# Changing where halves of weights are made and dealt in a gMLP, attention and PEER block on one core

## The chip, the cores and the metric

The kernel runs on one core of a Trainium2 chip. The metric is the device time of one execution in microseconds (us). Names used below: PE is TensorE (matmuls), DVE is VectorE, ACT is ScalarE, POOL is GpSimd, SP is the engine that issues most loads. Each engine works through a queue of its own in order, and engines wait for one another by semaphores. SBUF is the memory on the chip, PSUM the banks that PE writes its products into.

## What is computed

For 512 tokens of width 1024 in float32:

```python
xn = rms_norm(x, ln_mix_g);  proj = xn @ w_in
a_out = gmlp_spatial_gating(proj[..., :512], proj[..., 512:1024], ...)
b_out = banded_chunk_attention(q, k, v, ...)          # 8 heads, chunks of 64
x = x + concatenate([a_out, b_out]) @ w_out
# PEER: 8 heads, 16 of 128 x 128 experts each
q = rms_norm(x) @ w_query;  sc = q . sub_keys         # two halves of the key
best, eidx = top 16 of the sums of the two top 16
g = softmax(best);  u = expert_u[eidx];  vv = expert_v[eidx]
x = x + sum(g * gelu(u . xn) * vv)
```

There are 16384 experts, and each token uses 8 x 16 of them.

## The kernel before

**Halves.** A float32 product is made of three matmuls of a shorter format. A weight tile of 128 x 1024 is loaded into `raw` (512 KB, SP's queue, three buffers), ACT copies it to `hi` (L157, five buffers), and DVE or POOL subtracts to get `lo` (L158, five buffers). `mm3` (L196 to L198) then multiplies hi by hi, hi by lo and lo by hi. `load_split` (L149) does load, copy and subtraction in one go; `Pieces` (L181) does the same for the first chunks of `w_in`, piece by piece (L140, L145, L146).

**Head.** The first chunk of `w_in` comes in four pieces. Three are loaded at the start (the `raw` buffers), the fourth after the second piece has been used. The product of token tile 0 goes over the pieces as they come (`product`, L339), while PE transposes token tile 1 (L292), DVE multiplies it with the gain (`xg`, L298) and ACT and DVE halve it (`xh` L303, `xl` L304). The first k-steps of tile 1 follow.

**PEER.** 384 of the 512 tokens don't gather their experts: for them the hidden product is made with all 16384 experts, and gates that are zero for all but the chosen ones are multiplied in. (64 of these tokens are handled by gathers all the same, early, in the gate stage; the remaining 128 tokens gather in the loop, spread over DVE and POOL.) The experts come in 128 tiles of 128.

- A *first product* is one tile of experts by 320 tokens: 8 k-steps of 3 matmuls into a PSUM bank (`pu`, two banks). ACT's gelu (L724) moves the bank to `act`. `multiply_some(n)` (L698) issues n k-steps, from a tile left open or from the list `ready`, which holds tiles whose halves have been issued; `HELD` is 2.
- A *second product* (L1171) takes two tiles of `vd` rows (64 chunks, c = 0 to 63) and the gated activations `wh`, `wl` into 6 PSUM banks (L1215). Ahead of it DVE multiplies the gates `gc` in (L1181), ACT and DVE halve the outcome (L1182, L1183).

**Gate stage** (L1029 to L1090, 438.6 to 584.2 us in the trace). The order of PE, DVE, ACT and POOL is written out by hand there. 48 steps of 8 tokens, with a lead of 2: in each step POOL makes `bm` (L981) from two digits `hb` and `lb` of the expert number, DVE makes `am` (L989), PE multiplies them for each token (L998: eight matmuls in the program, 16 records in the trace), ACT copies the four-token results out of two PSUM banks (`gst`, L1001) and, each second step, stores them (`gd`, L1005, 1024 KB). `digits` (L963) makes `hb` (a one-hot, L970, times the gate, L973) and `lb` (L970) for 16 tokens at a time. From step 6 to step 32, in seven steps of eight, POOL also gathers rows for the 64 tokens (`rowe`, L660) and DVE multiplies and sums them (L670). Behind the gate matmuls of a step, `some` k-steps of first products are issued: what is left by then, divided by the steps that are left. At the end of a step the halves of the next tile are issued in one go (load, copy, subtraction; every fourth subtraction on POOL), while `ready` holds fewer than two.

**Loop** (L1225 on). For each c the second product of c and the two first products of c + 25 are issued, and every third c the routing of the gathered tokens on DVE. PE's order is by hand; the other engines' order is set by a scheduler by priority. Only `queued_behind` and `issue_after` tie an instruction to another one's place.

## Time and profile before

| what | value |
|---|---|
| median of three runs | 1411.17 us (1410.4 to 1411.97) |
| the profiled execution | 1410.74 us |
| its span on the core | 1409.0 us |
| granted TensorE clock | 0.999 |
| PE busy | 1386.7 us (98%) |
| DVE busy | 1154.3 us (82%) |
| POOL busy | 673.0 us (48%) |
| ACT busy | 612.0 us (43%) |
| DMA | 396.24 MB, mean 281 GB/s |

The span runs from the first to the last instruction, and all times of rows count from its start. In a timeline a row has the start, the duration, engine, line of the kernel before, operation, what it writes and reads, and in brackets the idle time of the engine ahead of it with what ended that. An x behind a row counts equal instructions in a run. Matmuls overlap, so the pitch between their starts is their price, not the duration.

### The profile page before, as it was taken

Reading aid. Unit: us, or ns where it says so; the run is one execution under the profiler, and the core shown is the slowest. Engines: PE = TensorE matmul, PEld = TensorE weight load, DVE = VectorE, ACT = ScalarE, POOL = GpSimd, SP = SyncE. Lnnn points to the kernel's source line nnn. Section 1 sums busy time; section 2 is a strip of 40 time slices with the busy share of each in tenths; the row PEclk is TensorE's granted clock in tenths of the full one; section 3 lists DMA queues with packets and bytes.
Section 4 is the critical chain, followed back from the end, with each engine's and each line's share of the span. In section 5 each row is a group of like instructions: output and inputs, shape, how many; then the busy total and the mean of one; then the engine's idle time right before and its main releaser. Section 6 shows DMA issues by size and latency. Waiting matters only on the chain.

```text
span 1409.0 us, 21692 instructions
## 1 busy us (share of the span) xinstructions
PE 1386.7 (98%) x7838; PEld 1224.6 (87%) x7838; DVE 1154.3 (82%) x2508; ACT 612.0 (43%) x960; POOL 673.0 (48%) x486
## 2 busy tenths in 40 slices
PE   9999999999999989999999999999999999999998
PEld 7887688899899989988898899899889989888887
DVE  5437845898998998678999999898898887889983
ACT  5447635443434445534344444444443333333331
POOL 0002103777778998424555456454464543344520
PEclk9999999999999999999999999999999999999999
DMA  4452316567666999979999999999999998799981
GB/s 165 135 194 76 104 72 199 193 220 271 240 225 222 348 354 281 289 254 355 330 342 348 362 360 342 369 372 359 375 348 383 352 359 337 272 353 363 357 311 60
DMA packets 164330, 396.24 MB, mean 281 GB/s; under 512 B 12880, under 2 KB 75232, under 8 KB 162176
## 3 DMA queue, kind: packets, MB, share of 16 engines
q1 hardware_dynamic: 64640, 194.14, 37.6%
q0 software_dynamic: 48176, 173.46, 33.9%
q10 hardware_dynamic: 51408, 27.27, 6.6%
q8 instruction: 61, 1.00, 0.3%
q14 instruction: 45, 0.37, 0.1%
HBM read 363.34 MB, written 31.46 MB: 280 GB/s over the span
## 4 chain that ended last, share of the span: by engine, by line
PE 78%; DVE 13%; DMA 2%; POOL 2%; issue 2%; ACT 2%; ACTq 0%; DVEq 0%; POOLq 0%
PE pa L1215 23%; PE px L1215 12%; PE pu L196 9%; PE pu L198 9%; PE pu L197 9%; PE pa L998 3%; PE pa L196 3%; PE pa L197 3%; PE pa L198 3%; DVE rowe L670 2%; DVE lo L158 2%; DVE tree L800 1%; DVE am L989 1%; DMA raw<-in_vd 1%; POOL rowe L660 1%
## 5 line engine op out<-in xcount | busy, mean ns | idle before, releaser
L157 ACT ACTIVATE hi<-raw 128x1024 fp32r<-128x1024 f32 x296 | 313.0, 1058 | 448.2 <-DMA raw<-in_uT 120.8
L158 DVE TENSOR_TENSOR lo<-raw,hi 128x1024 fp32r<-128x1024 f32 x244 | 305.7, 1254 | 99.9 <-ACT hi L157 99.1
L1139 POOL DMA_INDIRECT row<-in_ud,eint x128 | 193.0, 1508 | 180.8 <-DVE acc L1152 129.4
L196 PE MATMUL pu<-xch,hi 128*128 128x320 f32 x784 | 247.5, 316 | 3.0 <-ACT act L724 2.8
L1150 POOL DMA_INDIRECT row<-in_vd,eint x128 | 159.7, 1247 | 178.0 <-DVE row L1141 118.6
L198 PE MATMUL pu<-xch,lo 128*128 128x320 f32 x784 | 242.8, 310 | 0.8 <-DVE lo L158 0.8
L197 PE MATMUL pu<-xcl,hi 128*128 128x320 f32 x784 | 242.8, 310 | 0.0
L1215 PE MATMUL pa<-lo,wh 128*128 128x512 f32 x512 | 199.7, 390 | 0.0
L1215 PE MATMUL pa<-hi,wh 128*128 128x512 f32 x512 | 199.4, 389 | 0.0
L158 POOL TENSOR_TENSOR lo<-raw,hi 128x1024 fp32r<-128x1024 f32 x52 | 124.0, 2398 | 119.0 <-ACT hi L157 116.1
L1152 DVE SCALAR_TENSOR_TENSOR acc<-row,hw,acc 128x1024 f32<-128x1024 f32 x128 | 165.2, 1290 | 2.8 <-DMA row<-in_vd,eint 2.5
L1141 DVE SCALAR_TENSOR_TENSOR row<-row,xb 128x1024 f32<-128x1024 f32 x128 | 155.7, 1220 | 10.3 <-DMA row<-in_ud,eint 10.3
L1215 PE MATMUL pa<-hi,wl 128*128 128x512 f32 x512 | 158.5, 389 | 0.0
L196 PEld LDWEIGHTS pu<-xch,hi 128*128 128x128 f32 x784 | 148.0, 189 | 6.1 <-ACT act L724 4.4
L197 PEld LDWEIGHTS pu<-xcl,hi 128*128 128x128 f32 x784 | 148.1, 189 | 1.4
L198 PEld LDWEIGHTS pu<-xch,lo 128*128 128x128 f32 x784 | 147.8, 189 | 1.1 <-DVE lo L158 1.0
L1215 PEld LDWEIGHTS pa<-hi,wh 128*128 128x128 f32 x512 | 96.1, 188 | 20.5
L1215 PEld LDWEIGHTS pa<-hi,wl 128*128 128x128 f32 x512 | 96.1, 188 | 20.3
L1215 PEld LDWEIGHTS pa<-lo,wh 128*128 128x128 f32 x512 | 96.1, 188 | 20.2
L998 PE MATMUL pa<-bm,am 128*128 128x128 f32 x768 | 95.1, 277 | 8.0 <-POOL bm L981 4.2
L998 PEld LDWEIGHTS pa<-bm,am 128*128 128x128 f32 x768 | 90.7, 191 | 11.7 <-POOL bm L981 6.5
L1215 PE MATMUL px<-hi,wh 128*128 128x512 f32 x256 | 100.1, 391 | 0.4 <-ACT hi L157 0.4
(236 smaller groups left out, 2641.6 us busy)
## 6 DMA issues: line engine op xcount, KB each, us to landing
raw<-in_uT SPq DMA_DIRECT2D x128, 512.0 KB
raw<-in_vd SPq DMA_DIRECT2D x128, 512.0 KB
gd<-gst ACTq DMA_DIRECT2D x24, 1024.0 KB
gc<-gd SPq DMA_DIRECT2D x15, 1280.0 KB
raw<-in_w_in SPq DMA_DIRECT2D x19, 512.0 KB
raw<-in_wq SPq DMA_DIRECT2D x16, 512.0 KB
raw<-in_w_out SPq DMA_DIRECT2D x8, 512.0 KB
gc<-gd SPq DMA_DIRECT2D x15, 256.0 KB
```

Of the source, the lines that this page charges most:

```text
L157: top = nc.scalar.activation(hi, raw, AF.Copy)
L158: ins = eng.tensor_tensor(lo, raw, hi.bitcast(F32), op=ALU.subtract)
L196: nc.tensor.matmul(ps, lh[0], rh[0], start=first, stop=False)
L197: nc.tensor.matmul(ps, lh[0], rh[1], start=False, stop=False)
L198: nc.tensor.matmul(ps, lh[1], rh[0], start=False, stop=last)
L670: nc.vector.scalar_tensor_tensor(row, row, 1.0, xbu, op0=ALU.mult, op1=ALU.mult, accum_out=du[:, j:j + 1])
L998: nc.tensor.matmul(ps[:, i * P:(i + 1) * P], am[:, 4 * q + i, :], bm[:, 4 * q + i, :], start=True, stop=True)
L1139: nc.gpsimd.indirect_dma_start(out=row, out_offset=None, in_=ud, in_offset=bass.IndirectOffsetOnAxis(ap=eint[:, j:j + 1], axis=0))
L1141: nc.vector.scalar_tensor_tensor(row, row, 1.0, xb0, op0=ALU.mult, op1=ALU.mult, accum_out=hw[:, j:j + 1])
L1150: nc.gpsimd.indirect_dma_start(out=row, out_offset=None, in_=vd, in_offset=bass.IndirectOffsetOnAxis(ap=eint[:, j:j + 1], axis=0))
L1152: nc.vector.scalar_tensor_tensor(acc0, row, hw[:, j:j + 1], acc0, op0=ALU.mult, op1=ALU.add)
L1215: nc.tensor.matmul(accs[t][half], (wh, wh, wl)[k][:, b, tok], w[b][k % 2][:, ds_], start=first and k == 0, stop=last and k == 2)
```

## The change

Four edits in one:

1. The fourth piece of the first `w_in` chunk goes into a raw buffer of its own (`raw3`), and its load is issued right behind that of token tile 1. The load of `qkgt` now comes later on SP's queue.
2. `digits` makes `hb` for 32 tokens in one pair of operations every second time; `lb` stays at 16.
3. In the gate stage a tile's load and copy are issued at the start of a step (`split_begun`), ahead of the gst copies on ACT, and its subtraction at the step's end. It is begun while `ready` holds at most two. The k-steps are dealt out by another formula: steps up to own - 5 (own is 40) count three times as much as those behind. Per step PE's first-product matmuls were 6 once, 9 ten times and 6 for 36 steps; they are now 6 once, 9 for 30 steps, 6 for five, 3 for four and none for the last seven.
4. In the loop each copy `hi` of a half is queued behind the gelu of the half five earlier, where that half was a first product's and its gelu was issued in the loop.

The diff, without the changes that only carry the new entry of a tuple along:

```diff
...
 AHEAD = 25
 LAST = 2
 HELD = 2
+LATE = 3
 EASY = 8
 SOME = 15
 FILL = (0, 1, 2, 3, 4, 4, 3, 3)
...
                        allow_small_or_imprecise_dtypes=True)
 
         loads, splits, ready = [], [], []
+        halves_of, gelus, looping = [0], {}, []
         roots, behind_scale, behind_norm, halved = [], [], [], []
 
         def queued_behind(marks):
...
                 ctx.enter_context(tc.issue_after(i))
             return ctx
 
-        def load_pieces(src, n, b):
-
-            raw, hi, lo = big("raw", F32, RAW), big("hi", F32R, HI), big("lo", F32R, LO)
+        def load_pieces(src, n, b, raw=None):
+
+            raw, hi, lo = raw or big("raw", F32, RAW), big("hi", F32R, HI), big("lo", F32R, LO)
             m = 1024 // n
             cs = [slice(i * m, (i + 1) * m) for i in range(n)]
             for i in range(n):
...
             fold = (lambda v: v.rearrange("p (a b) -> p a b", **dims)) if dims else (lambda v: v)
             load = nc.sync.dma_start(fold(raw), src)
             loads[:] = [getattr(load, "ins", load)]
-            top = nc.scalar.activation(hi, raw, AF.Copy)
+            halves_of[0] += 1
+            with queued_behind(gelus.get(halves_of[0] - HI, [])):
+                top = nc.scalar.activation(hi, raw, AF.Copy)
             ins = eng.tensor_tensor(lo, raw, hi.bitcast(F32), op=ALU.subtract)
             halved[:] = [getattr(i, "ins", i) for i in (top, ins)]
             if eng is nc.gpsimd:
                 splits[:] = [getattr(ins, "ins", ins)]
             return fold(hi), fold(lo)
 
+        def split_begun(i):
+
+            raw, hi, lo = big("raw", F32, RAW), big("hi", F32R, HI), big("lo", F32R, LO)
+            load = nc.sync.dma_start(raw.rearrange("p (a b) -> p a b", b=P), uT[i].rearrange("p (a b) -> p a b", b=P))
+            loads[:] = [getattr(load, "ins", load)]
+            halves_of[0] += 1
+            n_ = halves_of[0]
+            nc.scalar.activation(hi, raw, AF.Copy)
+
+            def finish(eng):
+                eng.tensor_tensor(lo, raw, hi.bitcast(F32), op=ALU.subtract)
+                ready.append((*divmod(i, BC), [v.rearrange("p (a b) -> p a b", b=P) for v in (hi, lo)], n_))
+            return finish
+
         def split_tile(i, eng):
 
-            ready.append((*divmod(i, BC), load_split(uT[i], eng, b=P)))
+            ready.append((*divmod(i, BC), load_split(uT[i], eng, b=P), halves_of[0]))
 
         def chunk_of(w, c, ch=CH, eng=nc.vector, ks=range(KT)):
 
...
             def __init__(self, w, c, first):
                 self.w, self.c, self.first, self.parts = w, c, first, {}
 
-            def load(self, j):
+            def load(self, j, raw=None):
                 self.parts[j] = load_pieces(self.w[2 * j * P:2 * (j + 1) * P, self.c * CW:(self.c + 1) * CW]
-                                            .rearrange("(k p) n -> p k n", p=P), 1 if j else self.first, CW)
+                                            .rearrange("(k p) n -> p k n", p=P), 1 if j else self.first, CW, raw)
 
             def split(self, j, i=0, n=2):
                 self.parts[j][1](i, n)
...
                 for j in range(3):
                     w_at.load(j)
                 nc.sync.dma_start(x_t[1], x_r[1])
+                w_at.load(3, prea.tile([P, D], F32, name="raw3", tag="xs", bufs=4))
                 ps0 = pu()
 
                 def product(t, ps, ks):
...
                 w_at.split(1, 0)
                 w_at.split(1, 1)
                 product(0, ps0, range(2, 4))
-                w_at.load(3)
                 w_at.split(2, 0)
                 w_at.split(2, 1)
                 scale_of(0)
...
         def activate_tile():
-            c, b, ps = begun.pop(0)
+            c, b, n_, ps = begun.pop(0)
             ins = nc.scalar.activation(acts[c][:, b, :], ps[:, :NDU], AF.Gelu_apprx_tanh)
             done[:] = [getattr(ins, "ins", ins)]
+            if looping:
+                gelus[n_] = list(done)
...
             nc.tensor.transpose(ps[:, 3 * P:4 * P], gate[:, t, :], ident)
             return ps.rearrange("p (a t) -> p a t", a=4)
 
+        high = []
+
         def digits(g, q):
 
-            ts_ = slice(q * QT, (q + 1) * QT)
-            hb = gp.tile([P, QT, BH], F32, name="hb", tag="hb", bufs=2)
-            lb = gp.tile([P, QT, BL], F32, name="lb", tag="lb", bufs=2)
-            for i, (d, n) in enumerate(((hb, BH), (lb, BL))):
-                full = [P, QT, n]
+            w = 2 * QT
+
+            def one_hot(name, i, n, ts_):
+                full = [P, ts_.stop - ts_.start, n]
+                d = gp.tile(full, F32, name=name, tag=name, bufs=2)
                 nc.vector.tensor_tensor(d, iota_k[:, None, 0:n].to_broadcast(full),
                                         g[:, 1 + i, ts_, None].to_broadcast(full), op=ALU.is_equal)
-                if i == 0:
-                    nc.vector.tensor_tensor(d, d, g[:, 3, ts_, None].to_broadcast(full), op=ALU.mult)
-            return hb, lb
+                return d
+
+            if q % 2 == 0:
+                ts_ = slice(q * QT, q * QT + w)
+                hb = one_hot("hb", 0, BH, ts_)
+                nc.vector.tensor_tensor(hb, hb, g[:, 3, ts_, None].to_broadcast([P, w, BH]), op=ALU.mult)
+                high[:] = [hb]
+            return high[0][:, q % 2 * QT:(q % 2 + 1) * QT], one_hot("lb", 1, BL, slice(q * QT, (q + 1) * QT))
 
         def second_one_hot(d, c):
 
...
             multiply_tile()
             for n in range(steps + LEAD):
                 t, c = divmod(n, per)
+                halved_now = []
+                if n > 1 and split < (AHEAD - LAST) * BC + HELD and len(ready) <= HELD and (n > EASY or n % 2 == 0):
+                    halved_now = [(split_begun(split), nc.vector if split % 4 else nc.gpsimd)]
+                    split += 1
                 if n < steps:
                     bms[n] = second_one_hot(dgs[n * TC // QT], c)
                 if n >= LEAD:
...
                     t1, c1 = divmod(n + 2, per)
                     dgs[(n + 2) * TC // QT] = digits(late if n + 2 >= own else gs[t1], c1 * TC // QT)
 
-                made = len(ready) * KT + (KT - open_tile[4] if open_tile else 0)
-                left = (AHEAD - LAST) * BC * KT - split * KT + made
-                some = -(-left // (steps + LEAD - n))
+                made = len(ready) * KT + (KT - open_tile[5] if open_tile else 0)
+                left = (AHEAD - LAST) * BC * KT - split * KT + made + len(halved_now) * KT
+                some = -(-left * LATE // (LATE * max(0, own - 5 - n) + min(steps + LEAD - n, steps + LEAD - own + 5)))
                 multiply_some(some)
-                if n > 1 and split < (AHEAD - LAST) * BC + HELD and len(ready) < HELD and (n > EASY or n % 2 == 0):
-                    split_next(nc.vector if split % 4 else nc.gpsimd)
+                for finish, eng in halved_now:
+                    finish(eng)
             while ready or open_tile:
                 if split == AHEAD * BC and not weights:
                     weights[0] = rows_of_v(0)
...
         acx = px()
         accs = [[acx[:, 0:512], acx[:, 512:]]] + [[pa() for _ in range(2)] for _ in range(ND - 1)]
         own_last = []
+
+        looping.append(True)
 
         def second_product(c, between):
             w = weights.pop(c) if c in weights else rows_of_v(c)
```

SP at the head of the program. raw tiles are pieces of `w_in`, x_t token tiles of x, qkgt two small gains. Before:

```order
L140 DMA raw_166<-in_w_in 128x2x512
L140 DMA raw_170<-in_w_in 128x2x512
L336 DMA x_t_114<-in_x 128x1024
L386 DMA qkgt_376<-in_qkg 128x2
L140 DMA raw_198<-in_w_in 128x2x512
L369 DMA x_t_115<-in_x 128x1024
```

After:

```order
L142 DMA raw_166<-in_w_in 128x2x512
L142 DMA raw_170<-in_w_in 128x2x512
L354 DMA x_t_114<-in_x 128x1024
L142 DMA raw3_175<-in_w_in 128x2x512
L387 DMA x_t_115<-in_x 128x1024
L387 DMA x_t_116<-in_x 128x1024
```

The fourth piece (raw_198, now raw3_175) stands right behind x_t_114, token tile 1; qkgt has gone behind the token tiles.

DVE in the middle of the gate stage, two steps. am and the digits hb, lb belong to the gates, rowe to the early gathers, lo to the next first products. Before:

```order
L970 TENSOR_TENSOR hb_5293<-iota_k_74,pa_5077 128x128
L973 TENSOR_TENSOR hb_5293<-hb_5293,pa_5077 128x128
L970 TENSOR_TENSOR lb_5294<-iota_k_74,pa_5077 128x256
L989 TENSOR_TENSOR am_5319<-iota_k_74,pa_5077 128x1024
L670 SCALAR_TENSOR_TENSOR rowe_5171,du_2091<-rowe_5171,px_2074 128x1024
L989 TENSOR_TENSOR am_5346<-iota_k_74,pa_5077 128x1024
L670 SCALAR_TENSOR_TENSOR rowe_5226,du_2091<-rowe_5226,px_2074 128x1024
L970 TENSOR_TENSOR hb_5351<-iota_k_74,pa_5077 128x128
L973 TENSOR_TENSOR hb_5351<-hb_5351,pa_5077 128x128
L970 TENSOR_TENSOR lb_5352<-iota_k_74,pa_5077 128x256
L158 TENSOR_TENSOR lo_5365<-raw_5363,hi_5364 128x1024
```

After:

```order
L992 TENSOR_TENSOR lb_5312<-iota_k_74,pa_5071 128x256
L178 TENSOR_TENSOR lo_5289<-raw_5287,hi_5288 128x1024
L1016 TENSOR_TENSOR am_5339<-iota_k_74,pa_5071 128x1024
L688 SCALAR_TENSOR_TENSOR rowe_5174,du_2091<-rowe_5174,px_2074 128x1024
L1016 TENSOR_TENSOR am_5376<-iota_k_74,pa_5071 128x1024
L688 SCALAR_TENSOR_TENSOR rowe_5240,du_2091<-rowe_5240,px_2074 128x1024
L992 TENSOR_TENSOR hb_5381<-iota_k_74,pa_5071 128x256
L999 TENSOR_TENSOR hb_5381<-hb_5381,pa_5071 128x256
L992 TENSOR_TENSOR lb_5384<-iota_k_74,pa_5071 128x256
L178 TENSOR_TENSOR lo_5357<-raw_5355,hi_5356 128x1024
```

The pair for hb stands in every second group, at twice the size, and in two steps there are two subtractions lo where there was one.

ACT in the loop, around the second product of c = 1 and the first products behind it. hi are copies of halves, act the gelus (pu is the PSUM bank that one frees), wh the halves of gated activations, top a step of the routing. Before:

```order
L1182 ACTIVATE wh_6707<-act_2859 128x2x320
L157 ACTIVATE hi_6576<-raw_6575 128x1024
L1195 ACTIVATE wh_6707<-gc_6065 128x4x2x16
L157 ACTIVATE hi_6626<-raw_6625 128x1024
L157 ACTIVATE hi_6659<-raw_6658 128x1024
L724 ACTIVATE act_6511<-pu_6510 128x320
L724 ACTIVATE act_6219<-pu_6245 128x320
L767 ACTIVATE top_7286<-pos_7287 128x16
L157 ACTIVATE hi_6696<-raw_6695 128x1024
```

After:

```order
L1215 ACTIVATE wh_6671<-act_2859 128x2x320
L161 ACTIVATE hi_6540<-raw_6539 128x1024
L1228 ACTIVATE wh_6671<-gc_6061 128x4x2x16
L161 ACTIVATE hi_6590<-raw_6589 128x1024
L742 ACTIVATE act_6475<-pu_6474 128x320
L161 ACTIVATE hi_6623<-raw_6622 128x1024
L742 ACTIVATE act_6183<-pu_6209 128x320
L742 ACTIVATE act_6475<-pu_6507 128x320
L161 ACTIVATE hi_6660<-raw_6659 128x1024
```

Of the two copies that stood together ahead of two gelus, the second (hi_6659, now hi_6623) stands behind the first gelu.

More of the change, by code (lines that the diff above doesn't have):

```diff
@@ L708, in multiply_some @@
                                                                           tag=f"act{slot}")
-                c, b, (hi, lo), ps, k0 = open_tile
+                c, b, (hi, lo), n_, ps, k0 = open_tile
                 k1 = min(KT, k0 + n)
@@ L713, in multiply_some @@
                 n -= k1 - k0
-                open_tile[4] = k1
+                open_tile[5] = k1
                 if k1 == KT:
-                    begun.append((c, b, ps))
+                    begun.append((c, b, n_, ps))
                     open_tile.clear()
```

## The prediction

> **What bounds the kernel now.** I read the page first, then the waits of TensorE, a table of windows over the stages, and last the timelines around the longest waits and around every place that the change touches.
>
> From the page, the busy time of each engine (PE is TensorE, PEld its weight loads, DVE VectorE, ACT ScalarE, POOL GpSimd; us, share, instructions) and the rate of the DMA by slice:
> ```profile
> PE 1386.7 (98%) x7838; PEld 1224.6 (87%) x7838; DVE 1154.3 (82%) x2508; ACT 612.0 (43%) x960; POOL 673.0 (48%) x486
> GB/s 165 135 194 76 104 72 199 193 220 271 240 225 222 348 354 281 289 254 355 330 342 348 362 360 342 369 372 359 375 348 383 352 359 337 272 353 363 357 311 60
> ```
> PE is busy for 98%, and the change leaves the number of matmuls alone. So it can only win idle time of PE, time at a low clock, or work that hides elsewhere. The longest wait of PE, from the view of its waits (us in total, times, longest):
> ```profile
> PE pu L196 <- ACT act L724: 3.0, 3, 2.0
> ```
> L196 is a first product, which waits until ScalarE's gelu has emptied a PSUM bank. Now the windows: the gate stage from the step where the new dealing of first products begins to differ (473.41) in two parts, the start of the loop over c, and the loop up to 765 us:
> ```profile
> 473.41:537.38 63.97, 57.41 (x451) 54.24 (x449) 63.09 (x99) 29.28 (x50) 60.81 (x39) 1.00 1.06 352
> 537.38:584.24 46.86, 45.42 (x373) 44.92 (x373) 32.47 (x50) 24.48 (x42) 34.90 (x19) 1.00 0.90 264
> 612.60:634.70 22.10, 20.08 (x100) 17.89 (x99) 18.57 (x65) 10.23 (x18) 10.24 (x5) 0.92 0.58 196
> 634.70:765.00 130.30, 130.30 (x710) 117.02 (x708) 126.10 (x325) 54.69 (x85) 67.75 (x48) 1.00 0.93 339
> ```
> Columns: length, then busy time of PE, PE's weight loads, DVE, ACT, POOL, then granted clock, DMA share, GB/s. Each stage has its own limit. In the first row, where the early gathers run, DVE is full (63.09 of 63.97), POOL nearly so (60.81), the DMA at a share of 1.06, and PE idles 6.6 us. In the second PE is the bound (45.42 of 46.86) and DVE and POOL have room. In the third PE idles 2 us and its clock falls to 0.92. In the fourth PE is full, but DVE has only 4.2 us to spare. The dealing moves PE work from the second row into the first: that is the core of the forecast.
>
> **The head: the fourth piece in a buffer of its own.** ScalarE, then VectorE, then PE:
> ```profile
> 13.93 1.15 ACT L145 ACTIVATE hi<-raw 128x512 fp32r<-128x512 f32 x2 [1.53 <-DMA raw<-in_w_in]
> ```
> ```profile
> 14.59 1.29 DVE L146 TENSOR_TENSOR lo<-raw,hi 128x512 fp32r<-128x512 f32 x2 [1.74 <-ACT hi L145]
> 15.80 1.28 DVE L298 TENSOR_TENSOR xg<-pa,g 128x512 f32<-128x512 f32 x2
> ```
> ```profile
> 13.11 1.04 PE L292 MATMUL pa<-ident,x_t 128*128 128x128 f32 x8
> 14.61 0.50 PE L196 MATMUL pu<-hi,xh 128*128 128x512 f32 x1 [0.46 <-ACT hi L145]
> ...
> 17.19 0.50 PE L196 MATMUL pu<-hi,xh 128*128 128x512 f32 x1 [0.44 <-ACT xh L303]
> ```
> The piece lands late, so its hi starts at 13.93 after 1.53 us of waiting, DVE makes lo at 14.59, and only behind that comes xg (15.80), then ScalarE's xh, for which the next product waits until 17.19. With its load issued ahead of the wait for a raw buffer, hi and lo fall before the transposes of 13.11 end (14.15). Then xg starts at about 14.15, and the product 1.39 behind it, as now, at 15.5: 17.19 less 15.5 is **-1.7 us**. It can't gain more than the waits of the chain, 1.53 + 0.46 or 2.0; it gains nothing if x_t[2] and x_t[3], now behind one more load on SP's queue, become what is late. I take 1.7, since those two are used a product later. qkgt, moved behind them too, is read after this product only.
>
> **The gate stage.** A step is 16 gate records and some first-product matmuls. Their prices, on PE:
> ```profile
> 443.22 0.31 PE L197 MATMUL pu<-xcl,hi 128*128 128x320 f32 x1
> 444.31 0.42 PE L198 MATMUL pu<-xch,lo 128*128 128x320 f32 x1 [0.78 <-DVE lo L158]
> 444.57 0.31 PE L196 MATMUL pu<-xch,hi 128*128 128x320 f32 x1
> ...
> 445.45 1.95 PE L998 MATMUL pa<-bm,am 128*128 128x128 f32 x16
> 447.15 0.40 PE L196 MATMUL pu<-xch,hi 128*128 128x320 f32 x1
> ```
> From 444.57 to 445.45 there are six first-product matmuls: 0.147 each. The gate records take 447.15 - 445.45 = 1.70. The code now deals 9 matmuls to each of 30 steps, 6 to five, 3 to four and none to seven; before it was 9 to ten and 6 to 36.
>
> *Begun halves.* hi ahead of the gst copies takes away the wait at 444.31: from 443.22 to 444.31 went 1.09 where 0.15 is the pitch. -0.9; it may gain nothing if lo, now at the end of a step, stays late. Behind the copy on ACT's queue now stand the gst copies, for which PE's gate matmuls wait; the copy is about 1.15 us long (the two halves of 13.93), PE has PSUM banks for two steps, and its raw tile is asked for as soon as a buffer comes free, tiles ahead. So I take nothing for it, up to 1 us a tile if that cover is gone.
>
> *Gather phase (473.41 to 537.38, 20 steps).* Three more matmuls a step are 60, or 8.8 us of PE work, where PE idles 6.6: by PE alone +2.2. But DVE is the fuller engine here. Its rows for this window, then POOL's around 507 and DVE's subtraction beside them:
> ```profile
> L158 DVE TENSOR_TENSOR lo<-raw,hi 128x1024 fp32r<-128x1024 f32 x5 | 9.4, 1877 | 0.0
> L970 DVE TENSOR_TENSOR lb<-iota_k,pa 128x256 f32<-128x256 f32 x10 | 4.1, 413 | 0.0
> L973 DVE TENSOR_TENSOR hb<-hb,pa 128x128 f32<-128x128 f32 x10 | 2.9, 287 | 0.3
> L970 DVE TENSOR_TENSOR hb<-iota_k,pa 128x128 f32<-128x128 f32 x10 | 2.8, 281 | 0.3 <-POOL bm L981 0.3
> ```
> ```profile
> 506.77 1.94 POOL L981 TENSOR_TENSOR bm<-hb,lb 128x1024 f32<-128x1024 f32 x1
> 508.87 1.80 POOL L660 DMA_INDIRECT rowe<-in_ud,eui  x1 [0.16 <-issue]
> ```
> ```profile
> 506.55 3.25 DVE L158 TENSOR_TENSOR lo<-raw,hi 128x1024 fp32r<-128x1024 f32 x1
> ```
> Sixty matmuls are 2.5 tiles more, so 2.5 more halves; three in four fall to DVE: 1.9 x 1.88 = 3.6 us. The digits give back: ten pairs cost 2.9 + 2.8 = 5.7, five pairs of double size at 0.413 each cost 4.1, so -1.6. DVE: +2.0. The DMA: 2.5 x 512 KB = 1.3 MB more at 352 GB/s is +3.7 if it is the limit, and nothing if it can go at the 383 that a later slice shows. Between +2.0 and +3.7 nothing tells them apart; I take **+2.8**.
>
> A half on DVE and a bm on POOL hold each other up: the lo of 506.55 took 3.25 beside the bm of 506.77, where two of half the size took 1.29 at 14.59, and the gather behind it, 508.87, took 1.80. The Trainium skill ("SBUF — State Buffer", "Who interferes with whom") says that a DVE operation with two SBUF inputs and a GpSimd operation take an exclusive lock on a shared port pair, and the loser is blocked to the end of the other; the trace agrees, 1.94 + 1.29 is 3.23. That speaks against three more matmuls a step here, and is a case of its own below.
>
> *Late steps (537.38 to 584.24, 16 steps).* 96 matmuls become 30 + 12 = 42: 54 x 0.147 = -7.9. Seven steps then have 1.70 of PE work, and POOL needs 1.94 for a bm (506.77), so +0.24 each, +1.7. Net -6.2. The 1.4 us of idle left there may go or stay.
>
> *Afterwards.* The gate steps hold 6 + 270 + 30 + 12 = 318 first-product matmuls instead of 312, so six fewer are left for later: -0.9.
>
> Gate stage: -0.9 + 2.8 - 6.2 - 0.9 = **-5.2 us**, from -8.9 (2.2 for the gather phase, and the 1.4 us gone as well) to about 0 (below).
>
> **The loop: halves behind gelus.** ScalarE and PE around the longest wait:
> ```profile
> 627.18 2.00 ACT L157 ACTIVATE hi<-raw 128x1024 fp32r<-128x1024 f32 x2 [1.83 <-issue]
> 629.09 0.74 ACT L724 ACTIVATE act<-pu 128x320 f32<-128x320 f32 x2
> ```
> ```profile
> 629.56 0.41 PE L196 MATMUL pu<-xch,hi 128*128 128x320 f32 x1 [2.02 <-ACT act L724]
> ...
> 631.46 0.47 PE L198 MATMUL pu<-xch,lo 128*128 128x320 f32 x1
> 631.72 0.47 PE L196 MATMUL pu<-xch,hi 128*128 128x320 f32 x1
> ```
> Two copies stand ahead of a gelu that PE waits for. With the gelu first, or between them, the 2.0 us go, and with them what follows: at 631.46 a matmul has a pitch of 0.26 instead of 0.147, for some 13 matmuls: 1.6 us more. Together -3.6.
>
> The page "TensorE: Matmul & The Clock Gate" of the Trainium skill (Part 1) puts the cold clock behind an idle window of about 3.4 us; here 2.0 us of idle went ahead of it. By that page the 1.6 would not hang on this wait and would stay; the forecast's sum would be the same, for the cap below is under 2.0, and the case without a cap 1401.6.
>
> The same place comes once more, with a table load:
> ```profile
> 763.07 1.06 ACT L157 ACTIVATE hi<-raw 128x1024 fp32r<-128x1024 f32 x1 [0.60 <-DMA raw<-in_uT]
> 764.15 1.28 ACT L724 ACT_TABLE_LOAD   x1
> ```
> ```profile
> 765.93 0.42 PE L196 MATMUL pu<-xch,hi 128*128 128x320 f32 x1 [0.73 <-ACT act L724]
> ```
> One copy leaves the place ahead of the load, 1.06 us, more than the 0.73. So -4.3 in sum. But this gain is PE's alone: DVE has 4.2 us to spare up to 765, and further on its subtraction reaches PE just in time:
> ```profile
> 782.97 1.22 DVE L158 TENSOR_TENSOR lo<-raw,hi 128x1024 fp32r<-128x1024 f32 x1
> ```
> ```profile
> 785.41 0.31 PE L198 MATMUL pu<-xch,lo 128*128 128x320 f32 x1
> ```
> lo ends at 784.19 and is read at 785.41: 1.2 us. What PE gains before 612 us moves DVE too, for there DVE follows PE; what it gains behind that can only use up this 1.2, plus a little that DVE's idle 3.5 us in 612.60 to 634.70 may give. I take **-1.5**, between 0 and -4.3. Put behind gelus, the copies come later by at most 0.74, the time of the two gelus of 629.09. Behind a copy stand on ACT the wh copies of the second product, for which DVE and PE wait; a gelu starts when its matmuls end, so they wait no longer than that either, and DVE's full queue covers it.
>
> **Sum:** -1.7 - 5.2 - 1.5 = -8.4. The profiled execution took 1410.74, its span and 1.7 us around it; it is 0.43 under the median of 1411.17. So 1402.3 against it, and **1402.8** as a median. About 0.2%, 2.8 us, is what a measurement can tell from no change.
>
> **The rivals.**
> - *No cap by DVE.* The loop gives all of -4.3: 1400.0. For: DVE's chain up to 634 waits for PE in places, and it may start earlier. Against: 126.10 of 130.30.
> - *The port holds the gather phase.* All subtractions that DVE then does there, three in four of 7.5 or 5.6, take 3.25: 18.2 instead of 9.4 us, less 1.6 of digits and 0.9 of DVE's idle time, +6.3 instead of +2.8: 1406.3. For: 506.55. Against: the mean of 1.88 says that about one in three meets a whole bm.
> - *The copies do nothing in the loop*: the waits move to the next gelu and stay. 1404.3.
> - *The gate stage gains nothing*: both limits add up, the port's 6.3 and the DMA's 3.7 less the 2.0 of DVE that is in both: +8.0 instead of +2.8, -3.2 in sum, 1408.0, or no change where the loop gains nothing either.
> - *Slower: the stores hold the gate results.* ScalarE's waits in the gather phase:
> ```profile
> ACT gst L1001 <- DMA gd<-gst: 4.2, 2, 3.0
> ```
> A copy out of PSUM waits for the store that has its buffer, twice, 2.1 each. With 1.3 MB more on a full DMA all ten stores of the phase could: 8 x 2.1 = +17, in place of +2.8: 1417. It decides against the kernel from 1.4 us a store on ((8.4 + 2.8) / 8). Against it: the loads asked for are 6% more bytes, and the DMA reached 383 GB/s.
>
> **How the numbers follow.** Chances: forecast 0.45, no cap 0.17, port 0.18, nothing in the loop 0.06, gate gains nothing 0.08, stores 0.06. The first four are faster by over 0.2%: 0.86. The fifth lies at the bound: 0.08 the same. The last is 0.06 slower. The range leaves out the stores and half of the fifth above, and below only the corner where every bound comes out good (-1.7 - 8.9 - 4.3 is 1396.3): 1397.0 to 1408.3.
>
> **What would show it.** Right: the product of 17.19 near 15.5; the part that was 473 to 537 some 3 us longer and the part behind it 6 to 7 shorter, first second-product matmul 6 to 8 us earlier; no wait of 2 us and clock 1.00 around 630; instead waits for lo L158 near 750 to 790. Wrong: gate steps over 3.4 us in the gather phase, waits of gst for gd in more than two places, or an idle stretch of PE ahead of the first second product, while gates are loaded.

## The result, and the profile after

The changed kernel took 1399.76 us (median of 4, 1397.34 to 1401.7) against 1411.57 us; the ratio is 0.991 (95% interval 0.9897 to 0.9923), 10.9 to 14.5 us less. In another group of runs it took 1400.74 against 1411.99, 0.9916 (0.99 to 0.9931). The forecast was 1402.8, from 1397.0 to 1408.3: the direction and the range hold, and the change is 3 us larger than the likeliest value. The profiled execution, at 1397.34, is the fastest of its four; where it matters, a second profile of the same kernel, of an execution of 1401.05, stands beside it.

The busy times and the longest waits of PE after:

```profile
PE 1381.2 (99%) x7838; PEld 1222.8 (88%) x7838; DVE 1154.7 (83%) x2484; ACT 615.5 (44%) x960; POOL 672.1 (48%) x486
```

```profile
PE pa L1025 <- DVE ff L909: 1.9, 1, 1.9
PE px L1248 <- ACT hi L161: 1.5, 1, 1.5
PE pu L214 <- ACT act L742: 1.2, 2, 0.8
```

Before, the longest in sum was the one for bm (us in total, times, longest):

```profile
PE pa L998 <- POOL bm L981: 4.2, 8, 1.2
```

The wait of 2.0 us for a gelu is gone, and 0.5 us is left of the 4.2 us for bm. Two waits have grown at their places: PE now waits 1.9 us for the indices ff ahead of the twelfth gate step, where it waited 0.4 (over the stage it is 1.9 in both, in two places before), and 1.5 us instead of 0.4 for a copy hi in the first second product. The gate stage after, cut at the same steps as before, and the place where PE waited at 630 us:

```profile
435.80:471.61 35.81, 33.89 (x275) 33.66 (x273) 33.57 (x44) 20.15 (x32) 33.73 (x22) 1.00 0.89 277
471.61:536.05 64.44, 63.59 (x508) 63.09 (x508) 64.13 (x88) 33.76 (x55) 61.59 (x38) 1.00 1.07 361
536.05:574.49 38.44, 37.78 (x319) 37.19 (x319) 28.08 (x38) 20.70 (x37) 31.83 (x18) 1.00 0.90 261
600.00:621.00 21.00, 20.94 (x117) 18.77 (x116) 18.03 (x65) 10.12 (x18) 7.92 (x4) 1.00 0.63 212
```

In the gather phase (second row) PE was busy for 57.41 of 63.97 us and is now for 63.59 of 64.44: 60 more matmuls were taken up for half a microsecond. Where the 13.7 us between the two spans come from, by the starts of the same instruction in both traces:

| stretch | before | after | difference | second profile | forecast |
|---|---|---|---|---|---|
| up to the first gate matmul | 438.62 | 435.80 | -2.8 | -1.7 | -1.7 |
| first 11 gate steps | 34.79 | 35.81 | +1.0 | +1.0 | -0.9 |
| gather phase, 20 steps | 63.97 | 64.44 | +0.5 | +0.6 | +2.8 |
| late steps, to the first second product | 54.27 | 46.60 | -7.7 | -7.6 | -6.2 |
| from there to the second product of c = 2 | 43.08 | 38.78 | -4.3 | -4.2 | -0.9 and part of -1.5 |
| the rest | 774.27 | 773.87 | -0.4 | +1.7 | part of -1.5 |

The two profiles of the changed kernel agree within 0.1 us on the four middle rows. They differ by 1.1 ahead of the gate stage and by 2.1 in the rest, so differences of that size there belong to the execution. The 1.1 is a wait named "issue" (L853 before, L873 after), which stands in the first trace of before and in the second of after, and is missing in the first of after.

### The profile page after: what moved, and what is told of

It is laid out like the page before. It is cut to its first block, busy times and chain, and to the rows that moved or that the text cites. A ratio compares the mean times of both kernels' runs of the same rounds, so it can differ in the third digit from the quotient of the medians.

```text
span 1395.3 us, 21679 instructions
## 1 busy us (share of the span) xinstructions
PE 1381.2 (99%) x7838; PEld 1222.8 (88%) x7838; DVE 1154.7 (83%) x2484; ACT 615.5 (44%) x960; POOL 672.1 (48%) x486
## 4 chain that ended last, share of the span: by engine, by line
PE 75%; DVE 14%; POOL 4%; issue 3%; DMA 2%; ACT 1%; ACTq 0%; POOLq 0%; DVEq 0%
PE pa L1248 24%; PE px L1248 12%; PE pu L216 8%; PE pu L214 8%; PE pu L215 8%; PE pa L1025 3%; PE pa L214 3%; DVE rowe L688 3%; PE pa L215 3%; PE pa L216 3%; POOL bm L1008 1%; POOL rowe L678 1%; DVE tree L820 1%; DMA raw<-in_uT 1%; DVE rep L762 1%
## 5 line engine op out<-in xcount | busy, mean ns | idle before, releaser
L161 ACT ACTIVATE hi<-raw 128x1024 fp32r<-128x1024 f32 x281 | 297.1, 1058 | 414.7 <-DMA raw<-in_uT 122.6
L162 DVE TENSOR_TENSOR lo<-raw,hi 128x1024 fp32r<-128x1024 f32 x232 | 284.1, 1226 | 81.2 <-ACT hi L161 80.9
L162 POOL TENSOR_TENSOR lo<-raw,hi 128x1024 fp32r<-128x1024 f32 x49 | 116.9, 2403 | 117.0 <-ACT hi L161 116.1
L1172 DVE SCALAR_TENSOR_TENSOR row<-row,xb 128x1024 f32<-128x1024 f32 x128 | 156.2, 1223 | 11.8 <-DMA row<-in_ud,eint 11.8
L1248 PE MATMUL px<-lo,wh 128*128 128x512 f32 x256 | 100.3, 392 | 0.0
L1008 POOL TENSOR_TENSOR bm<-hb,lb 128x1024 f32<-128x1024 f32 x48 | 93.8, 1964 | 6.0 <-PE pa L1025 3.3
```

What stands on the lines that cost most here:

```text
L161: top = nc.scalar.activation(hi, raw, AF.Copy)
L162: ins = eng.tensor_tensor(lo, raw, hi.bitcast(F32), op=ALU.subtract)
L1008: nc.gpsimd.tensor_tensor(bm.rearrange("p t (h l) -> p t h l", l=BL), d[0][:, ts_, :, None].to_broadcast(full), d[1][:, ts_, None, :].to_b ...
L1172: nc.vector.scalar_tensor_tensor(row, row, 1.0, xb0, op0=ALU.mult, op1=ALU.mult, accum_out=hw[:, j:j + 1])
L1248: nc.tensor.matmul(accs[t][half], (wh, wh, wl)[k][:, b, tok], w[b][k % 2][:, ds_], start=first and k == 0, stop=last and k == 2)
```

## The experiments

Three groups of four kernels, each group on one chip with its own runs of the kernel before. The theory was first that the parts add, each where it acts; the rival was that a later bound swallows what an earlier stage gains.

**One part alone** (before: 1412.7, 25 runs).

*The fourth piece alone.*

```diff
+                w_at.load(3, prea.tile([P, D], F32, name="raw3", tag="xs", bufs=4))
...
-                w_at.load(3)
```

> The kernel before with only the fourth piece in a raw buffer of its own. Theory 1 (the gains of the parts add, each keeps what it wins in its own place): the first product of token tile 1 comes 1.5 us earlier and the whole time falls by 1.5 us (1410 to 1409.5). Theory 2 (what an early stage gains is swallowed by the next stage that has another bound): the product comes 1.5 earlier, the whole falls by less than 0.5.

1410.33; ratio 0.9981 (0.9971 to 0.9992), -1.1 to -4.1 us. Faster beyond the interval, and 1.5 lies in it. In its trace the shift after the head is 1.6 up to 320 us and still 1.4 to 1.5 from the gate stage to 630. Its span, 1408.7, is hardly shorter than before's, since in that execution PE waited longer for gelus in the loop: 6.1 us against 3.0.

*The digits alone.*

```diff
+            if q % 2 == 0:
+                ts_ = slice(q * QT, q * QT + w)
+                hb = one_hot("hb", 0, BH, ts_)
```

> The kernel before with only hb made for 32 tokens at a time. DVE is full in the gather phase (473 to 537 us) and loses 1.6 us of work there. Theory 1: the gather phase is bound by DVE, -1.0 to -1.6. Theory 2: it is bound by POOL or the DMA as well, 0 to -0.5.

1412.49; ratio 1.0 (0.9989 to 1.0011). Nothing, so what DVE saves there is lost before the end. In the trace the gather phase is 1.6 us shorter, and the shift is gone by 730 us: at 718 PE waits 1.99 us for a gelu, where before doesn't wait, and the clock is about 0.67 up to 723 us. The kernel with the fourth piece alone waits there too, 1.72 us. So in these two executions a part of what was gained early is lost to a later wait for ScalarE, which is the rival's case.

*The gate stage alone* (halves begun and new dealing, without the digits):

```diff
+                if n > 1 and split < (AHEAD - LAST) * BC + HELD and len(ready) <= HELD and (n > EASY or n % 2 == 0):
+                    halved_now = [(split_begun(split), nc.vector if split % 4 else nc.gpsimd)]
...
+                some = -(-left * LATE // (LATE * max(0, own - 5 - n) + min(steps + LEAD - n, steps + LEAD - own + 5)))
```

> The kernel before with only the gate stage's new order (halves begun at the start of a step, first products dealt out anew), with the old digits, the old head and the old loop. Theory 1: -1.0 from the begun halves, +2.5 in the gather phase (3 more matmuls a step, no relief by digits), -6 in the late steps, -0.9 afterwards: -5.4. Theory 2 (the digits are what makes room for the extra matmuls): the gather phase costs +5 or more, the whole -3 or less.

1404.14; ratio 0.9935 (0.9921 to 0.995), -7.1 to -11.2 us: more than the forecast's terms for it, and without the digits. One reason is that this kernel, with the old order in the loop, has no wait near 616 us, where 630 was before. Theory 2 falls.

*The queueing alone.*

```diff
-            top = nc.scalar.activation(hi, raw, AF.Copy)
+            with queued_behind(gelus.get(halves_of[0] - HI, [])):
+                top = nc.scalar.activation(hi, raw, AF.Copy)
```

> The kernel before with only the copies of the loop queued behind gelus. Theory 1 (the gain of the loop is whole, DVE follows): the 2.0 us wait and the half clock at 630 and the wait at 766 go, -3.5 to -4.3. Theory 2 (DVE caps it, as forecast): PE then waits for lo near 750 to 790, the whole -1.2 to -2.

1409.51; ratio 0.9972 (0.9962 to 0.9983), -2.4 to -5.4 us. By the time alone this would be theory 1, but its trace says something else. PE's waits between 600 and 800 us:

```profile
PE pu L214 <- ACT act L742: 2.0, 2, 1.1
PE pu L216 <- DVE lo L162: 0.8, 1, 0.8
```

The wait for the gelu near 630 is halved to 1.1, not gone, and a wait for lo has come in. Neither theory as put; the profiled execution is also the slowest of its eight. The four parts alone add up to 14.3 us by their medians, the whole change is 11.3 to 11.8: they nearly add, and what is missing is within the intervals.

**One part left out** (before: 1411.99, 14 runs).

*The changed kernel again*, without an edit.

> The changed kernel once more, on the chip of the runs beside it: -11.8 us against before. If the waits in the loop are settled by the order alone, its profile shows the same ones as the first (ScalarE's hi near 588, a gelu near 756); if they depend on the execution, others.

1400.74; ratio 0.9916 (0.99 to 0.9931). The copy hi near 588 is waited for in both profiles (1.5 and 1.6); a wait for lo near 712 stands only in the second, a longer one for the gelu near 759 too:

```profile
712.09 0.42 PE L216 MATMUL pu<-xch,lo 128*128 128x320 f32 x1 [0.84 <-DVE lo L162]
```

```profile
759.31 0.41 PE L214 MATMUL pu<-xch,hi 128*128 128x320 f32 x1 [0.95 <-ACT act L742]
```

*Without the queueing* (the copy of load_split as before).

> The changed kernel without the queueing of copies behind gelus. Theory 1 (as forecast, the queueing takes the 2.0 us wait near 630 away): the wait is back, the whole 1.5 to 3.5 slower than the changed kernel. Theory 2 (the new dealing already takes it away, since nine matmuls of another tile now stand between the gelu's tile and the next, as the kernel with the gate stage alone shows): no wait near 613 to 621, within 0.7 of the changed kernel.

1403.65; ratio 0.9941 (0.9924 to 0.9957), 2.9 us above the changed kernel beside it, though the two intervals overlap a little. Both theories are half right: no wait near 620, as theory 2 said, and slower, as theory 1 said. The price lies further on: against the second profile of the changed kernel this trace is 0.1 us late at 736 and 1.7 from 776 on. ACT, then PE:

```profile
753.34 1.06 ACT L160 ACTIVATE hi<-raw 128x1024 fp32r<-128x1024 f32 x1 [1.16 <-DMA raw<-in_uT]
754.42 1.28 ACT L741 ACT_TABLE_LOAD   x1
```

```profile
756.20 0.41 PE L213 MATMUL pu<-xch,hi 128*128 128x320 f32 x1 [1.81 <-ACT act L741]
```

A copy that waits for its load stands ahead of the table load and the gelu, and PE waits 1.81 us: the picture that before shows at 763 to 766 with 0.73. With the queueing the copy stands behind the gelu, and 0.4 to 0.95 is left.

*Without the digits* (hb for 16 tokens at a time).

> The changed kernel with hb made for 16 tokens at a time again. Theory 1 (DVE bounds the gather phase, which now holds more): 1.0 to 1.6 slower than the changed kernel, and the gather phase longer by that. Theory 2 (slack is taken up elsewhere, as with the digits alone): within 0.5.

1401.03; ratio 0.9919 (0.9905 to 0.9934). Theory 2: the digits are worth nothing that can be measured, here too. The gather phase takes 64.46 us, 64.44 with the digits, and PE is busy for 63.73 of it: PE is full there as well by now.

*Even dealing, halves begun early.*

```diff
-LATE = 3
+LATE = 1
```

> The changed kernel with LATE = 1: halves begun early, but first products dealt out evenly over the steps again. Theory 1 (the gain of the gate stage comes from late steps that POOL and PE then share): 4 to 6 slower than the changed kernel. Theory 2 (it comes from the halves begun early, which take PE's waits away in any dealing): less than 2 slower.

1408.54; ratio 0.9972 (0.9961 to 0.9983), 7.8 us above the changed kernel. Theory 1, and by more than it said. From step 37 to the first second product it takes 38.59 us where the changed kernel takes 32.23.

**What the gate stage hangs on** (before: 1412.29, 23 runs; the changed kernel isn't in this group, so ratios are compared).

*New dealing, halves issued together at the step's end.*

```diff
-                for finish, eng in halved_now:
-                    finish(eng)
+                if n > 1 and split < (AHEAD - LAST) * BC + HELD and len(ready) < HELD and (n > EASY or n % 2 == 0):
+                    split_next(nc.vector if split % 4 else nc.gpsimd)
```

> The changed kernel with its dealing, but with load, copy and subtraction of a half issued together at the end of a step again. Theory 1 (what the begun halves win, 1.05 us at the third step, is given back 30 us later, where PE waits 1.9 us for the indices ff behind a subtraction that POOL blocks for 5.2 us): within 0.7 of the changed kernel, and the wait for ff shorter than 1.9. Theory 2 (the gain is kept): 1.0 or more slower.

1408.71; ratio 0.9981 (0.997 to 0.9991), 9 to 10 us worse than with begun halves. The first theory is wrong by far: the begun halves don't win where I had looked (the third step), yet without them nearly all that the dealing brings is lost, 7.6 us of it in the first 36 gate steps (below).

*The first gates loaded two steps earlier.*

```diff
-                if n == steps - 2:
+                if n == steps - 4:
                     load_gates(0, nc.gpsimd, range(1))
```

> The changed kernel with the load of the first gates issued two steps earlier on POOL. Theory 1 (the new wait of PE in the first second product, 1.5 us for a copy hi near 588, comes from DVE, which stands 8.6 us for the gates with the subtractions queued behind, which hold the raw buffers): DVE's wait is 3 to 4 us shorter, PE's wait goes, 1.0 to 1.5 faster than the changed kernel. Theory 2 (the load waits for the stores and the DMA, not for its issue): the gates land when they did, no change.

1402.17; ratio 0.993 (0.9916 to 0.9945): no gain. The gates do come earlier, and PE's wait is 1.54 us as it was; see below for what it is.

*Four subtractions of the loop on POOL.*

```diff
-                    split_tile(j, eng)
+                    split_tile(j, nc.gpsimd if j in (58, 62, 66, 70) else eng)
```

> The changed kernel with four subtractions of the loop (tiles 58, 62, 66 and 70) on POOL instead of DVE. Theory 1 (DVE caps what PE gains up to 720 us): the wait for lo near 710 goes, 0.5 to 1.0 faster than the changed kernel. Theory 2 (POOL's gathers and ScalarE's queue take its place): no change or slower.

1407.98; ratio 0.9964 (0.9951 to 0.9978), some 7 us worse than the changed kernel. PE's waits between 570 and 800 us:

```profile
PE pu L216 <- DVE lo L162: 5.4, 4, 2.0
```

POOL has time there, but these subtractions stand in its queue among gathers. The waits for lo became longer. It doesn't test the cap cleanly, since it brings a delay of its own.

*A dealing between.*

```diff
-LATE = 3
+LATE = 2
```

> The changed kernel with LATE = 2, a dealing between the even one and the changed one. Theory 1 (the more first products lie in the gather phase the better, as long as DVE and the DMA take them): 1.5 to 4 slower than the changed kernel, which is 7.8 faster than the even one. Theory 2 (POOL's pace in the late steps already costs what the dealing brings): equal or up to 1 faster.

1409.84; ratio 0.998 (0.9971 to 0.999). Worse than theory 1 allowed, and no better than the even one. That, with the kernel without begun halves, showed that something else than the dealing decides.

**What it is.** Compare the stretch from the first gate matmul to step 37, by when the early gathers are summed: the kernel before, the changed one, the even one, and LATE = 2:

```profile
438.62:553.20 114.58, 105.79 (x836) 101.86 (x835) 107.71 (x166) 56.55 (x95) 105.07 (x64) 1.00 0.97 313
```

```profile
435.80:550.42 114.62, 111.61 (x896) 110.64 (x895) 111.58 (x151) 60.83 (x100) 108.39 (x66) 1.00 1.00 326
```

```profile
437.32:552.08 114.76, 105.52 (x836) 101.82 (x835) 112.05 (x148) 57.29 (x95) 107.02 (x66) 1.00 0.97 317
```

```profile
437.20:559.73 122.53, 113.21 (x881) 111.29 (x880) 119.77 (x151) 60.69 (x99) 108.65 (x66) 0.98 0.95 309
```

The first three take 114.6 to 114.8 us, with 246, 306 and 246 first-product matmuls dealt to them. So 60 matmuls, 8.8 us of PE work, cost nothing there. DVE's queue sets the pace by its busy time, with POOL the next (105 to 108), and what PE is dealt beside it is free until PE is full. The kernel with the digits alone bears that out: 1.6 us less work for DVE, and the gather phase is 1.6 shorter. LATE = 2 deals 291 and takes 8 us longer, with DVE busy for 119.77. DVE has no more to do; one kind of operation lasts longer. DVE and POOL of that kernel:

```profile
535.51 6.03 DVE L178 TENSOR_TENSOR lo<-raw,hi 128x1024 fp32r<-128x1024 f32 x1
```

```profile
534.75 5.70 POOL L1008 TENSOR_TENSOR bm<-hb,lb 128x1024 f32<-128x1024 f32 x3
```

A subtraction that takes 1.22 us by itself stands for 6.03. POOL's three products bm end at 540.45, and 1.09 later it is done. The same without begun halves:

```profile
538.59 6.10 DVE L162 TENSOR_TENSOR lo<-raw,hi 128x1024 fp32r<-128x1024 f32 x1 [0.18 <-ACT hi L161]
```

```profile
536.01 7.59 POOL L1008 TENSOR_TENSOR bm<-hb,lb 128x1024 f32<-128x1024 f32 x4
```

These subtractions waited for the whole row of bm, not only for the one that they met. It isn't always so. In the kernel before, DVE, then POOL:

```profile
442.18 2.08 DVE L158 TENSOR_TENSOR lo<-raw,hi 128x1024 fp32r<-128x1024 f32 x1 [1.14 <-ACT hi L157]
```

```profile
441.25 4.80 POOL L981 TENSOR_TENSOR bm<-hb,lb 128x1024 f32<-128x1024 f32 x2
```

Here the subtraction ended at 444.26, 1.1 us behind the first product (443.18), and the second one was drawn out by it: the two take 4.80 us, where two in a row take 3.81 in the changed kernel (458.58). The even kernel has such a case at 547.09 (2.11 us), the one without begun halves has two (439.69 and 463.22). What decides between the two outcomes isn't known from these runs. Summed over the gate stage, what subtractions lasted beyond 1.22 us is 6.4 before, 9.7 in the changed kernel, 8.2 with even dealing, 11.1 without begun halves and 17.6 with LATE = 2. In the last two kernels long ones (one of 4.9; two of 4.8 and 3.3) fall where POOL has no gathers between its bm any more, from about step 31 on, and where the gates of the last tokens wait for DVE. Up to step 37 the kernel without begun halves takes 122.19 us, like LATE = 2. The two also show granted clocks of 0.97 and 0.98 over this stretch, worth at most 2 to 4 of their 8 us. That the long subtractions are the cause is read from the rows; no kernel here moves one subtraction alone.

So I take the changed kernel for a good draw as well as a better plan: its worst meeting with a row of bm comes early (next section), and none from step 31 on.

## Why the prediction was right, and where it was not

**Head (-1.7): right.** The product that was at 17.19 starts at 15.73, and the shift is 1.5 in the first profile, 1.6 with this part alone.

```profile
15.73 0.50 PE L214 MATMUL pu<-hi,xh 128*128 128x512 f32 x1
```

**Begun halves (-0.9): right at its place, gone 30 us later.** The 1.05 us at the third step are won in every kernel with begun halves. Ahead of the twelfth step PE then waits. DVE, POOL and PE of the changed kernel:

```profile
458.26 5.23 DVE L178 TENSOR_TENSOR lo<-raw,hi 128x1024 fp32r<-128x1024 f32 x1
...
470.90 0.56 DVE L909 CAST ff<-pa 128x384 f32<-128x384 int32 x1
```

```profile
456.23 2.40 POOL L178 TENSOR_TENSOR lo<-raw,hi 128x1024 fp32r<-128x1024 f32 x1
458.58 3.81 POOL L1008 TENSOR_TENSOR bm<-hb,lb 128x1024 f32<-128x1024 f32 x2
```

```profile
471.61 0.35 PE L1025 MATMUL pa<-bm,am 128*128 128x128 f32 x1 [1.92 <-DVE ff L909]
```

The subtraction at 458.26 begins beside the end of POOL's own subtraction, is held up by the two bm behind that as well, and lasts 5.23 instead of 1.22. DVE's whole queue is later by that, and with it ff, for which PE waited 0.4 before and waits 1.9 now. The forecast looked only at the wait that the edit removes and didn't ask what is late next. The step that failed is "-0.9", which came out as +1.0; the worth of begun halves lies elsewhere, as shown by the kernel without them.

**Gather phase (+2.8): too dear; it was +0.5.** I had put the price between DVE (+2.0) and the DMA (+3.7). The DMA took 361 GB/s where it had moved 352, so 352 was no limit. DVE is full in both (63.09 of 63.97, 64.13 of 64.44), but its work rose by 1.0 only, not 2.0: the digits gave their 1.6, and the subtractions took 2.9 more than before, one more in place of the 1.9 forecast:

```profile
L178 DVE TENSOR_TENSOR lo<-raw,hi 128x1024 fp32r<-128x1024 f32 x6 | 12.3, 2046 | 0.0
```

The forecast's bound by PE alone, +2.2, was misread too. It took the 6.6 us of idle for all the room that PE had. But a step with six first products takes 2.67 us where nothing waits (569.20 to 571.87 before), so 20 of them are 53.4 of the 57.41 us that PE was busy; with nine it takes 3.11, in all 62.2. PE had 10.6 us of room for the 8.8, and is now nearly full.

The port case, +6.3, did not come about in this dealing; LATE = 2 shows that it could. Its sentence from the Trainium skill ("SBUF — State Buffer", "Who interferes with whom") is borne out in kind, an exclusive lock with a blocked loser. Its price can be larger than the page's words give it: the subtraction of 6.03 us was held up for 4.8 by three bm in a row, where the one that it met would have cost at most 1.9.

**Late steps (-6.2): right in kind, -8.4 in size** (46.86 to 38.44). The step that failed is the price of 54 x 0.147: a block of six matmuls between gate steps takes 0.97 (440.32 to 441.29 before) and one of three 0.53, since the change between the two kinds costs too; 16 blocks of six against five and four of three are -8.5. The last eight steps, without first products, take 14.90 where 1.70 each would be 13.6: +1.3, which I put down to POOL's pace; the forecast had it at 1.7. Idle time fell from 1.4 to 0.7. The first second product starts 9.0 us earlier; the forecast said 6 to 8.

**Loop (-1.5): size near, reasons wrong.** The wait of 2.0 us at 630 is gone, but the gate stage's new dealing took it away, not the queueing: the kernel with the gate stage alone and the one without the queueing don't have it, the one with the queueing alone has half of it. ACT and PE of the changed kernel there:

```profile
616.37 1.06 ACT L161 ACTIVATE hi<-raw 128x1024 fp32r<-128x1024 f32 x1 [1.99 <-issue]
617.34 0.42 ACT L742 ACTIVATE act<-pu 128x320 f32<-128x320 f32 x1
617.65 1.05 ACT L161 ACTIVATE hi<-raw 128x1024 fp32r<-128x1024 f32 x1
```

```profile
617.44 0.31 PE L216 MATMUL pu<-xch,lo 128*128 128x320 f32 x1
617.80 0.41 PE L214 MATMUL pu<-xch,hi 128*128 128x320 f32 x1
```

One copy still stands ahead of the gelu, behind the same wait of ACT for "issue". What saves PE is the block of 57 matmuls in place of 50: nine of them, from another tile, now lie between the gelu's tile and the next one, where two did. I had read the order of ACT and not counted what PE has in between.

Of the 3.6 us that I gave to this place, 1.6 was a matter of the execution. In the kernel with the fourth piece alone the same wait is followed by a full clock (ACT, PE, and the window):

```profile
625.77 2.00 ACT L157 ACTIVATE hi<-raw 128x1024 fp32r<-128x1024 f32 x2 [1.84 <-issue]
```

```profile
628.15 0.41 PE L196 MATMUL pu<-xch,hi 128*128 128x320 f32 x1 [2.02 <-ACT act L724]
```

```profile
611.00:633.20 22.20, 20.18 (x108) 17.77 (x107) 18.58 (x65) 10.23 (x18) 9.90 (x6) 1.00 0.56 194
```

The clock was 0.92 in the same window of before; with the digits alone it stayed full there too, and yet in that execution the wait of 1.99 us at 718 is followed by a low clock. So the half clock doesn't follow each such wait. The page "TensorE: Matmul & The Clock Gate" of the Trainium skill (Part 1) says that the window that is watched runs freely, which would explain the chance; that cause is not shown here.

**The cap by DVE: half right.** A wait for lo of 0.4 to 1.0 us near 712 to 723 stands in the second profile and in six more kernels with the queueing (and longer ones where subtractions went to POOL), not in the first profile. The place was off by some 40 us. It limits the loop, but by less than the 2.8 us that I took off for it. That it is DVE's pace was argued from its busy share; the one try to relieve it brought a delay of its own, so it isn't shown by an experiment.

**A new wait that the forecast had only as a sign.** It named an idle stretch ahead of the first second product, while gates are loaded. It came a little behind, 1.5 us at 587.6, and the gates aren't its cause. ACT, SP and PE of the changed kernel:

```profile
575.38 3.08 ACTq L1032 DMA_DIRECT2D gd<-gst  x1
578.51 2.01 ACT L161 ACTIVATE hi<-raw 128x1024 fp32r<-128x1024 f32 x2 [3.15 <-issue]
...
586.52 1.06 ACT L161 ACTIVATE hi<-raw 128x1024 fp32r<-128x1024 f32 x1 [2.25 <-DMA raw<-in_vd]
```

```profile
580.86 0.33 SPq L157 DMA_DIRECT2D raw<-in_vd  x1
```

```profile
587.63 0.50 PE L1248 MATMUL px<-hi,wh 128*128 128x512 f32 x1 [1.54 <-ACT hi L161]
```

Issuing the last store holds ACT for 3.08 us, 1.47 before. Two copies stand behind that, then their subtractions, and only these free the raw buffer for the load of 580.86. With the gates loaded earlier, DVE waited 5.5 us for them instead of 8.6, and the store and the copy were as late:

```profile
576.45 3.27 ACTq L1032 DMA_DIRECT2D gd<-gst  x1
579.76 2.01 ACT L161 ACTIVATE hi<-raw 128x1024 fp32r<-128x1024 f32 x2 [3.34 <-issue]
...
587.80 1.06 ACT L161 ACTIVATE hi<-raw 128x1024 fp32r<-128x1024 f32 x1 [2.27 <-DMA raw<-in_vd]
```

That rules the gates out; the chain from the store's issue is read from the timeline and was not undone by an experiment. Why the issue takes 3.1 us, with stores now every 4 us, stays open.

**The slower rival**, copies of gst waiting for their stores, did not come: in the gather phase there is no such wait any more (4.2 us before).

**The sum.** Terms of the wrong sign at the start (+1.9 us against the begun halves) and too dear in the gather phase (-2.3) nearly cancel, which is luck. The late steps and the first products that follow came as worked out or a little better, and the loop up to c = 2 gave more than the cap let me write down: of its 4.3, 1.6 is eleven first products fewer (the block ahead of the first second product has five more), and the rest is mostly the wait and the half clock of before at 630, less 1.2 of the new wait at 587.6. In the second profile, which is nearer its median, 1.7 of that is lost again in the rest. The measured median is that of the rival without a cap (1400.0), but not by its reasons: the wait near 630, 3.6 of its 4.3, went with the dealing, and what the queueing is worth in the changed kernel (2.9 by the medians) lies near 756. The best case given for the gate stage, -8.9, doesn't come out of its terms either: with +2.2 in the gather phase and the 1.4 gone it is -7.2, and with 2.2 taken off it is -8.8.

## What to carry to other kernels

Deal the work of an engine that has idle time to the stage where another engine sets the pace: there it is free until the first engine is full, and each piece dealt later costs its whole time. Before crediting a wait that an edit removes, find the next thing that the waiting engine needs, and count what stands between the two instructions on that engine's own queue. And a plan of this kind is only as good as its meetings: in this kernel, DVE subtractions with two SBUF inputs that met rows of GpSimd products went with up to 8 us between two dealings, so try the neighbouring dealings before judging an idea by one of them.

## What the runs showed of the hardware

- A DVE subtraction of 128 x 1024 with both inputs in SBUF, 1.22 us by itself, lasted 5.23, 6.03 and 6.10 us beside rows of three, three and four GpSimd operations, and ended about 1.1 us behind the last of them. In other meetings it got in behind the first of two products (2.08 us).
- A wait of 2.0 us on PE (627.5 to 629.56 before) was followed, 1.4 us later, by 3.4 us at a clock of 0.51 in one execution, and by a full clock in two others with the same wait at the same place.
- DMA queues moved 361 GB/s in a stretch that looked saturated at 352.
